# A two-layer encoder trunk: the scan, the projections and attention issued in the order in which the program emits them

## The chip, the cores and the metric

One core of a Trainium2 chip runs the whole program. The metric is the device time of one execution in microseconds (us), taken as the median of three runs. The core has four engines that compute, each with its own queue of instructions: TensorE (PE, matrix products and transposes), VectorE (DVE), ScalarE (ACT) and GpSimd (POOL). SyncE (SP) issues most DMAs.

## The reference

The kernel computes two layers of a streaming encoder on one sequence of 1024 tokens, model width 1024, in float32. What matters of one layer:

```
h    = rms_norm(x) * (1 + sc1) + sh1                # modulation: c_act @ ada_w
proj = h @ w_in                                      # 1024 x 3232, q, k, v and the inputs of the scan
attn = diff_attention(rotary(q), rotary(k), v)       # 4 heads, two softmaxes each, block-causal
rwkv = rwkv7_time_mix(proj[..., 1536:])              # 8 heads of 64, state scan over 1024 steps
x    = x + gt1 * (concat(attn, rwkv) @ w_out)
x    = x + gt2 * hier_moe(rms_norm(x)*(1+sc2)+sh2)   # 32 experts, top 2 of one group
```

The scan is `state = state*w + (state@a)*b + v*k`, `y = state@r`. A final RMSNorm follows the second layer.

## The kernel before

Each layer has two parts. The second part (the experts) is not touched. The first part, `phase_a`, holds the projections, the scan and attention, and is written as a set of generators ("agents") that a small planner, `weave`, steps through.

- The planner keeps a clock. An agent's step emits some instructions and yields two numbers: how much TensorE time the step takes, and how long the agent is to rest afterwards. A yield can also name an event (`"step", n`, `"F", 0`, `"H"`) that the agent waits for. At each turn the planner takes the first agent by rank whose rest is over. Ranks: the scan's second half 0 to 3 (`rwkv_back`, `rwkv_mid`, `rwkv_front`), the solve of the small triangular systems and the scan's first half 4 (`rwkv_first`), turning of q, k and v 5, the projections of the scan 6 (`project`), the modulation of later blocks 7 (`tables`), attention 8, the projections of q, k and v 9 (`head_qkv`).
- The planner charges only TensorE's time. What VectorE and ScalarE take enters as rests (`GAP_R`, `GAP_F`, `GAP_B`, `GAP_S` and so on), as far as a yield stands there.
- The order of emission is not yet the order on the engines. The framework has a scheduler of its own, which runs a timeline by its own cost estimates and puts each engine's instructions in the order in which it finds them ready. Before the change it does so with everything that `weave` emits. In the experts' part, and only there, the helper `in_order` (line 69) chains what it encloses.

Three places are spoken of later:

- A tile of projection weights. `split_w` (line 339) loads 512 KB into `wa_raw`, casts it on ScalarE to `wa_hi` (line 346) and writes the remainder `wa_lo` on VectorE (line 347). `proj_cm` (line 351) then runs, for each of eight blocks of rows, three matmuls: `wa_hi` with `hh`, `wa_hi` with `hl`, `wa_lo` with `hh` (lines 359 to 361), for each half of the tokens. Each finished product is taken out of PSUM by ScalarE: line 1069 for q, k and v, lines 371, 375 and 376 for the inputs of the scan. `wa_hi` and `wa_lo` have two buffers, `wa_raw` one. In `head_qkv` and in `project` no rest stands between the emission of the cast and that of the first matmul.
- The modulation, `ada_ps` (line 238): 512 KB of `ada_w` a step, two buffers, loaded by SP.
- VectorE instructions whose operand comes from a DMA that is issued in the same step: `lam_v` (line 1004, once a layer) and `g2` (line 1279, once a layer, after the load of `n2g` in line 1278).

Of the kernel before, what the change touches and what calls it, by code (L numbers as in the profile page):

```python
# [52 lines left out]
class Trunk:  # L53
# [329 lines left out]
    def weave(self):  # L383

        inf, agents = float("inf"), self.agents

        def ready(x):
            return self.when.get(x, inf) if isinstance(x, (str, tuple)) else x  # L390

        while agents:
            for x in agents:
                if ready(x[2]) <= self.clock:
                    break
            else:
                t = min(ready(x[2]) for x in agents)
                assert t < inf, [x[2] for x in agents]
                self.clock = t
                continue  # L400
            r = next(x[1], None)
            if r is None:
                agents.remove(x)
            elif isinstance(r, tuple) and not isinstance(r[0], str):
                self.clock += r[0]
                x[2] = self.clock + r[1]
            else:
                x[2] = r
# [1590 lines left out]
```

## Time and profile before

| | us |
|---|---|
| runs | 2683.93, 2695.6, 2697.16; median 2695.6 |
| the profiled execution | 2686.03 |
| its span | 2684.2 |
| PE busy | 2370.9 (88%) |
| DVE busy | 1848.7 (69%) |
| ACT busy | 1200.7 (45%) |
| POOL busy | 313.9 (12%) |

Read it by stages. The stretches from 140 to 870 us and from 1450 to 2150 us lie in the first part of the first and of the second layer, where `weave` has emitted the work; the experts run from about 1005 to 1340 and from 2278 to 2613 us. A share of the whole span mixes the two. A wait is the idle time of an engine ahead of an instruction, put down to what ended it. The granted clock of TensorE has two levels, 1.2 and 2.4 GHz; the profile gives its mean as a share of full speed, so 0.50 is the lower level throughout.

### The profile page before, as it was taken

How to read it: one execution, taken by the hardware profiler on the slowest of the kernel's cores; microseconds unless marked ns; L12 is line 12 of the kernel's file. 1: busy time of each engine (PE TensorE's matmuls, PEld its weight loads, DVE VectorE, ACT ScalarE, POOL GpSimd, SP SyncE). 2: the span in 40 equal slices, each digit the busy share in tenths (PEclk: the TensorE clock that was granted, in tenths of full speed). 3: DMA queues.
4: the chain of work that ended last, by engine and by line, in shares of the span. 5: the costliest groups of instructions: out<-in, count | busy, mean ns of one | idle time of the engine just before them, and what ended most of it. 6: DMA issues, size and time to landing. Idle time of an engine off the chain costs nothing. (4 is left out here: it accounts for less than half of the span.)

```text
span 2684.2 us, 45428 instructions
## 1 busy us (share of the span) xinstructions
PE 2370.9 (88%) x17313; PEld 1812.1 (68%) x17313; DVE 1848.7 (69%) x4045; ACT 1200.7 (45%) x2324; POOL 313.9 (12%) x251
## 2 busy tenths in 40 slices
PE   5998998898889969999959989889987996999992
PEld 3676666677767867776737767677776885677771
DVE  3357767656588477877764679965658847887775
ACT  5344443334266225555544545434426622555552
POOL 3000000000000012333310000000000001333330
PEclk8999888889989979999979989899988997999996
DMA  8476665535263258999952434445436234899985
GB/s 300 155 248 201 203 208 164 162 105 143 85 198 100 92 200 293 352 336 363 347 195 80 155 121 134 143 148 156 121 87 204 90 108 186 325 388 348 336 307 201
DMA packets 262789, 542.70 MB, mean 202 GB/s; under 512 B 76376, under 2 KB 180768, under 8 KB 232608
## 3 DMA queue, kind: packets, MB, share of 16 engines
q1 hardware_dynamic: 234560, 484.61, 53.7%
q0 software_dynamic: 23376, 40.99, 4.1%
q10 hardware_dynamic: 4624, 14.06, 1.4%
q8 instruction: 142, 2.33, 0.4%
q14 instruction: 87, 0.71, 0.1%
HBM read 459.29 MB, written 120.09 MB: 216 GB/s over the span
## 5 line engine op out<-in xcount | busy, mean ns | idle before, releaser
L1643 DVE TENSOR_TENSOR w_lo<-w_gu,w_hi 128x2048 fp32r<-128x2048 f32 x134 | 306.4, 2286 | 69.5 <-ACT w_hi L1642 69.3
L1642 ACT CAST w_hi<-w_gu 128x2048 fp32r<-128x2048 f32 x134 | 255.7, 1908 | 211.5 <-PE h_ps L1695 198.3
L359 PE MATMUL pj<-hh,wa_hi 128*128 128x512 f32 x800 | 332.5, 416 | 3.4 <-ACT wa_hi L346 3.1
L360 PE MATMUL pj<-hl,wa_hi 128*128 128x512 f32 x800 | 328.7, 411 | 1.5 <-DVE hl L336 1.4
L361 PE MATMUL pj<-hh,wa_lo 128*128 128x512 f32 x800 | 322.7, 405 | 3.7 <-DVE wa_lo L347 3.6
L1734 PE MATMUL y_ps<-w_d,hT 128*128 128x512 f32 x560 | 252.3, 593 | 3.4 <-ACTq L1795 2.4
L1694 PE MATMUL h_ps<-w_hi,xT_hi 128*128 128x512 f32 x560 | 242.9, 434 | 4.4 <-ACT xT_hi L1678 4.4
L1695 PE MATMUL h_ps<-w_hi,xT_lo 128*128 128x512 f32 x560 | 222.3, 397 | 2.5 <-DVE xT_lo L1679 2.5
L1696 PE MATMUL h_ps<-w_lo,xT_hi 128*128 128x512 f32 x560 | 222.2, 397 | 0.0
L1723 POOL DMA_INDIRECT yd<-yo,idx_s x70 | 183.6, 2624 | 290.2 <-DVE yo L1720 275.4
L359 PEld LDWEIGHTS pj<-hh,wa_hi 128*128 128x128 f32 x800 | 154.2, 193 | 42.9 <-issue 6.3
L361 PEld LDWEIGHTS pj<-hh,wa_lo 128*128 128x128 f32 x800 | 153.7, 192 | 39.6 <-DVE wa_lo L347 5.9
L360 PEld LDWEIGHTS pj<-hl,wa_hi 128*128 128x128 f32 x800 | 154.3, 193 | 36.1 <-issue 3.9
L1734 PEld LDWEIGHTS y_ps<-w_d,hT 128*128 128x128 f32 x560 | 100.9, 190 | 104.8 <-issue 100.4
L1694 PEld LDWEIGHTS h_ps<-w_hi,xT_hi 128*128 128x128 f32 x560 | 107.2, 191 | 38.1 <-issue 11.5
L1695 PEld LDWEIGHTS h_ps<-w_hi,xT_lo 128*128 128x128 f32 x560 | 107.2, 191 | 36.5 <-DVE th L1686 11.5
L1679 DVE TENSOR_TENSOR xT_lo<-xT_ps,xT_hi 128x1024 fp32r<-128x1024 f32 x70 | 85.7, 1225 | 64.8 <-ACT xT_hi L1678 64.8
L1696 PEld LDWEIGHTS h_ps<-w_lo,xT_hi 128*128 128x128 f32 x560 | 106.8, 191 | 23.0
L1720 DVE SCALAR_TENSOR_TENSOR yo<-y_ps,wsl,gt 128x1024 f32<-128x1024 f32 x70 | 89.9, 1284 | 38.3 <-PE y_ps L1734 38.3
L1189 ACT ACTIVATE at_p<-at_s,at_mx 128x256 f32<-128x256 f32 (+7 forms) x128 | 94.9, 741 | 39.0 <-DVE at_mx L1187 38.4
L1187 DVE TENSOR_REDUCE at_mx<-at_s 128x1 f32<-128x256 f32 (+7 forms) x128 | 95.9, 753 | 17.6 <-PE at_s L1185 16.4
L238 PE MATMUL ada_ps<-ada_w,crep 128*32 128x128 f32 x1536 | 70.2, 310 | 41.0 <-DMA ada_w<-in_ada_w 40.9
(436 smaller groups left out, 4934.0 us busy)
## 6 DMA issues: line engine op xcount, KB each, us to landing
w_gu<-in_moe_w_gu SPq DMA_DIRECT2D x140, 1024.0 KB
w_d<-in_moe_w_down SPq DMA_DIRECT2D x70, 1024.0 KB
ada_w<-in_ada_w SPq DMA_DIRECT2D x80, 512.0 KB
wa_raw<-in_w_in SPq DMA_DIRECT2D x50, 512.0 KB
sp_z<-z SPq DMA_DIRECT2D x32, 768.0 KB
b_zz<-sp_z SPq DMA_DIRECT2D x32, 512.0 KB
cy<-yd SPq DMA_DIRECT2D x16, 1024.0 KB
qkv<-qst SPq DMA_DIRECT2D x48, 256.0 KB
```

The costliest lines, as they stand in the source:

```text
L359: nc.tensor.matmul(ps, hi[:, k, :], self.hh[k][:, sl], start=(k == 0), stop=False)
L360: nc.tensor.matmul(ps, hi[:, k, :], self.hl[k][:, sl], start=False, stop=False)
L361: nc.tensor.matmul(ps, lo[:, k, :], self.hh[k][:, sl], start=False, stop=(k == NK - 1))
L1187: nc.vector.tensor_reduce(mx, ps[:, 0:n], axis=AX.X, op=OP.max, negate=True)
L1189: nc.scalar.activation(pm[:, 0:n], ps[:, 0:n], AF.Exp, bias=mx, accum_out=hs["s"][:, t, m:m + 1])
L1642: self.nc.scalar.copy(hi, raw)
L1643: eng.tensor_tensor(lo, raw, hi.bitcast(F32), op=OP.subtract)
L1694: nc.tensor.matmul(ph, hi[:, k, :], whi[:, k % 4, :], start=(k == 0), stop=False)
L1695: nc.tensor.matmul(ph, lo[:, k, :], whi[:, k % 4, :], start=False, stop=False)
L1696: nc.tensor.matmul(ph, hi[:, k, :], wlo[:, k % 4, :], start=False, stop=(k == NK - 1))
L1723: st = nc.gpsimd.indirect_dma_start(out=self.yd, out_offset=bass.IndirectOffsetOnAxis(ap=self.idx_s[:, e:e + 1], axis=0), in_=yos[e % 2], ...
L1734: nc.tensor.matmul(po[:, 512 * half:512 * half + 512], hT[:, k, :], w[:, k, 512 * half:512 * half + 512], start=(k == 0), stop=(k == 1))
```

## The change

Each step of an agent is now taken inside `in_order`, with one record of the last instruction of each engine for the whole of `weave`. Every instruction that a step emits on TensorE, ScalarE, VectorE or GpSimd (DMAs issued by ScalarE and GpSimd among them) gets an ordering edge from the one emitted before it on the same engine. Edges without a semaphore: they add no wait by themselves, they take away the scheduler's choice. SP's queue is not chained, nor is what is emitted before `weave` starts or after it ends.

```diff
-        inf, agents = float("inf"), self.agents
+        inf, agents, self.issued = float("inf"), self.agents, {}
...
-            r = next(x[1], None)
+            with self.in_order(self.issued):
+                r = next(x[1], None)
```

The helper, which both kernels have:

```
    def in_order(self, last):
        engines = [e.engine for e in (self.nc.tensor, self.nc.scalar, self.nc.vector, self.nc.gpsimd)]
        traced = self.nc.cur_bb.bb.instructions
        n = len(traced)
        yield
        for i in traced[n:]:
            if i.engine in engines:
                if i.engine in last:
                    self.tc.add_manual_dep(i, last[i.engine].name, ...)
                last[i.engine] = i
```

Nearly all of TensorE's rows in the first part change place. Lines behind 387 have a number higher by one in the changed kernel. In the rows below a name's last number tells one tile from another of the same name.

ScalarE, first layer, around the cast of the weight tile `wa_hi_6706` (for one of attention's projections). `pj` is the product of a projection in PSUM, `qst` its copy; `at_` is attention, `b_` and `rb_` the scan. Before:

```order
L925 ACTIVATE b_sq_5762<-b_y_5405 128x512
L820 COPY b_tt_5616<-rb_t_5821 32x4x32
L861 COPY b_gg_5790<-rb_m_5792 128x2x64
L346 CAST wa_hi_6706<-wa_raw_6704 128x1024
L1069 ACTIVATE qst_6064<-pj_5865 128x512
L1208 COPY at_wt_6814<-at_t_6815 128x384
L1189 ACTIVATE at_p0_6677,at_sum_6270<-at_s_6671,at_mx0_6675 128x512
```

After:

```order
L821 COPY b_tt_6453<-rb_t_6657 32x4x32
L1190 ACTIVATE at_p0_6677,at_sum_6270<-at_s_6671,at_mx0_6675 128x512
L1070 ACTIVATE qst_6701<-pj_6322 128x512
L346 CAST wa_hi_6706<-wa_raw_6704 128x1024
L1190 ACTIVATE at_p1_6720,at_sum_6270<-at_s_6714,at_mx1_6718 128x512
L840 COPY b_e_6360<-rb_w_6728 128x256
L1029 COPY qst_6739<-qk_t_6740 128x512
```

Before, the cast stands ahead of the copy of an earlier product (`pj_5865`), among work of the scan, with nothing of its own tile's turn in front of it. Now the cast stands directly behind the copy of `pj_6322`, the product that precedes its own use.

TensorE at the first use of the same tile. Before:

```order
L1185 MATMUL at_s_7517<-at_l0_5836,at_q0_6037 128x512
L902 MATMUL rb_y_6338<-b_sb_4417,b_dr_6017 64x128 x4
L908 MATMUL rb_y_6338<-b_e_5784,b_zz_6015 64x64 x16
L804 MATMUL rb_q_6367<-b_tt_6233,b_aa_6231 32x32 x8
L359 MATMUL pj_6710<-hh0_355,wa_hi_6706 128x512
L360 MATMUL pj_6710<-hl0_363,wa_hi_6706 128x512
L361 MATMUL pj_6710<-hh0_355,wa_lo_6707 128x512
L359 MATMUL pj_6710<-hh1_356,wa_hi_6706 128x512
```

After:

```order
L361 MATMUL pj_6322<-hh6_361,wa_lo_6070 128x512
L894 MATMUL rb_s_6693<-b_sb_4417,b_dr_6364 64x64 x2
L359 MATMUL pj_6322<-hh7_362,wa_hi_6069 128x512
L360 MATMUL pj_6322<-hl7_370,wa_hi_6069 128x512
L361 MATMUL pj_6322<-hh7_362,wa_lo_6070 128x512
L359 MATMUL pj_6710<-hh0_355,wa_hi_6706 128x512
L360 MATMUL pj_6710<-hl0_363,wa_hi_6706 128x512
L361 MATMUL pj_6710<-hh0_355,wa_lo_6707 128x512
L1183 MATMUL at_s_6714<-at_k1_5889,at_q1_6109 128x512
```

Before, other work stands ahead of the first matmul with `wa_hi_6706`. Now the last matmul of `pj_6322`, which ScalarE's copy waits for, is the row just ahead of the first matmul that needs the cast behind that copy.

VectorE, first layer, around `g2`, whose operand `n2g` a DMA of the same step brings; `at_mx` are the maxima that attention's exponentials need. Before:

```order
L109 SCALAR_TENSOR_TENSOR rs_y_sub_8606<-rs_u_sub_8607,rs_y_sub_8606 128x4
L107 SCALAR_TENSOR_TENSOR rs_u_sub_8607<-rs_v_sub_8605,rs_y_sub_8606 128x4
L1187 TENSOR_REDUCE at_mx0_8761<-at_s_8755 128x1
L108 TENSOR_TENSOR rs_u_sub_8607<-rs_u_sub_8607,rs_y_sub_8606 128x4
L1196 RECIPROCAL at_rec_8531<-at_sum_8530 128x2
L109 SCALAR_TENSOR_TENSOR rs_y_sub_8606<-rs_u_sub_8607,rs_y_sub_8606 128x4
L1197 SCALAR_TENSOR_TENSOR at_g_8532<-at_sum_8530,nlam_5587,at_rec_8531 128x1
L107 SCALAR_TENSOR_TENSOR rs_u_sub_8607<-rs_v_sub_8605,rs_y_sub_8606 128x4
L1198 SCALAR_TENSOR_TENSOR at_p0_8718<-at_p1_8738,at_g_8532,at_p0_8718 128x512
L108 TENSOR_TENSOR rs_u_sub_8607<-rs_u_sub_8607,rs_y_sub_8606 128x4
```

After:

```order
L109 SCALAR_TENSOR_TENSOR rs_y_sub_8606<-rs_u_sub_8607,rs_y_sub_8606 128x4
L1224 SCALAR_TENSOR_TENSOR at_ob_8425<-at_ob_8425,rs_y_sub_8606,subg_5590 128x128 x4
L1280 SCALAR_TENSOR_TENSOR g2_8652<-g2_8652,n2g_8653 128x1024
L1197 RECIPROCAL at_rec_8531<-at_sum_8530 128x2
L1198 SCALAR_TENSOR_TENSOR at_g_8532<-at_sum_8530,nlam_5587,at_rec_8531 128x1
L1199 SCALAR_TENSOR_TENSOR at_p0_8583<-at_p1_8591,at_g_8532,at_p0_8583 128x256
L1188 TENSOR_REDUCE at_mx0_8686<-at_s_8682 128x1
```

Both stand among attention's instructions. Before, the scheduler has put `g2` where it found the load done, and the maxima `at_mx0_8761` and others ahead of it; now `g2` stands where its step emits it, and the maxima `at_mx0_8686` and all later ones stand behind it.

## Rows read from the trace of the kernel before

**Rows 1.** The page, part 1: busy us, share, instructions.
```profile
PE 2370.9 (88%) x17313; PEld 1812.1 (68%) x17313; DVE 1848.7 (69%) x4045; ACT 1200.7 (45%) x2324; POOL 313.9 (12%) x251
```

**Rows 2.** Windows: stretch, length, busy PE, PEld, DVE, ACT, POOL, clock, DMA, GB/s.
```profile
140.00:870.00 730.00, 651.53 (x6301) 512.84 (x6294) 502.02 (x1424) 318.48 (x815) 11.48 (x27) 0.91 0.54 165
1450.00:2150.00 700.00, 630.59 (x5568) 502.09 (x5567) 507.52 (x1427) 331.94 (x843) 5.74 (x16) 0.93 0.44 132
```

**Rows 3.** Waits of PE, 140 to 870: us in total, times, longest.
```profile
PE rb_s L893 <- DVE b_sb L895: 16.8, 13, 6.7
PE ada_ps L238 <- DMA ada_w<-in_ada_w: 13.2, 11, 3.4
...
PE pj L361 <- DVE wa_lo L347: 3.6, 2, 3.1
...
PE pj L359 <- ACT wa_hi L346: 0.9, 1, 0.9
```

**Rows 4.** Waits of PE, 1450 to 2200.
```profile
PE pj L359 <- ACT wa_hi L346: 2.1, 1, 2.1
```

**Rows 5.** What writes and reads the weight tile: duration ns min/median/max, first and last start.
```profile
L347 DVE TENSOR_TENSOR wa_lo<-wa_raw,wa_hi x50: 1192/1224/1227, 35.1 to 1944.0; 128x1024 fp32r<-128x1024 f32 x50
L346 ACT CAST wa_hi<-wa_raw x46: 1027/1047/1058, 75.8 to 1942.9; 128x1024 fp32r<-128x1024 f32 x46
```

**Rows 6.** Groups of ACT by line, 140 to 870: busy us, mean ns, idle before.
```profile
L1069 ACT ACTIVATE qst<-pj 128x512 f32<-128x512 f32 x24 | 14.3, 597 | 34.0 <-PE pj L361 34.0
L375 ACT ACTIVATE krv<-pj,omu 128x511 f32<-128x511 f32 x9 | 6.1, 682 | 0.0
...
L376 ACT ACTIVATE krv<-pj,carry,omu 128x1 f32<-128x1 f32 x9 | 3.1, 347 | 0.5 <-DVE carry L373 0.5
```

**Rows 7.** Timeline of PE: start, us, instruction, idle before and what ended it.
```profile
229.81 0.49 PE L361 MATMUL pj<-hh,wa_lo 128*128 128x512 f32 x1 [3.12 <-DVE wa_lo L347]
...
230.37 0.40 PE L360 MATMUL pj<-hl,wa_hi 128*128 128x512 f32 x1
230.60 0.40 PE L361 MATMUL pj<-hh,wa_lo 128*128 128x512 f32 x1
...
266.73 1.08 PE L238 MATMUL ada_ps<-ada_w,crep 128*32 128x128 f32 x16 [3.44 <-DMA ada_w<-in_ada_w]
...
1550.26 0.50 PE L359 MATMUL pj<-hh,wa_hi 128*128 128x512 f32 x1 [2.12 <-ACT wa_hi L346]
...
1603.52 0.64 PE L804 MATMUL rb_q<-b_tt,b_aa 32*32 32x32 f32 x16 [2.65 <-DMA b_tt<-tinv]
```

**Rows 8.** Windows behind these waits: columns as in rows 2.
```profile
231.30:234.70 3.40, 3.40 (x10) 2.64 (x9) 3.33 (x11) 1.92 (x7) 0.00 (x0) 0.50 0.57 219
...
1550.30:1554.00 3.70, 3.65 (x15) 2.69 (x16) 3.08 (x7) 2.86 (x5) 0.00 (x0) 1.00 0.33 117
1603.50:1606.90 3.40, 3.38 (x36) 2.91 (x37) 2.08 (x4) 1.63 (x5) 0.00 (x0) 0.50 0.83 245
...
265.50:272.30 6.80, 5.57 (x42) 4.24 (x43) 3.98 (x13) 0.42 (x2) 0.00 (x0) 0.50 1.00 334
```

**Rows 9.** Timeline of SP, two issues of loads of modulation weights.
```profile
260.93 1.04 SPq L235 DMA_DIRECT2D ada_w<-in_ada_w  x2
```

**Rows 10.** Timeline of SP, the load that the second operand of g2 comes by.
```profile
795.49 0.42 SPq L1278 DMA_DIRECT2D n2g<-in_norm_g  x1
```

**Rows 11.** Timeline of DVE: two instructions behind a DMA of their own step.
```profile
801.73 1.23 DVE L1279 SCALAR_TENSOR_TENSOR g<-g,n2g 128x1024 f32<-128x1024 f32 x1 [0.85 <-DMA n2g<-in_norm_g]
...
1768.57 0.29 DVE L1004 TENSOR_TENSOR lam_v<-lam_v 128x128 f32<-128x128 f32 x1 [4.74 <-DMA lam_v<-in_attn_lambda]
```

**Rows 12.** Windows in which the scan's second half runs: columns as in rows 2.
```profile
374.00:700.00 326.00, 286.54 (x3267) 230.73 (x3260) 210.76 (x651) 117.05 (x307) 1.72 (x5) 0.86 0.48 144
...
1600.00:1975.00 375.00, 341.52 (x3628) 270.61 (x3627) 273.13 (x823) 158.90 (x403) 3.92 (x9) 0.94 0.48 142
```

## The prediction

> **What bounds the kernel now.** I read four views in this order. The page's busy shares come first: TensorE is busy for 88% of the span, VectorE for 69% [rows 1]. The windows then say where there is time to win or lose. In the two stretches that the change touches TensorE is busy 651.5 of 730 us and 630.6 of 700 us, so it idles for 78.5 + 69.4 = 147.9 us, and its mean clock is 0.91 and 0.93 [rows 2]. VectorE is at 69 and 73% there, ScalarE at 44 and 47%. TensorE bounds these stretches, but not without holes. Third, the waits: no single one dominates, the largest of the first layer being the scan's state step (16.8 us in 13 waits) and the modulation's loads (13.2 us in 11) [rows 3]. What matters most is a wait that is nearly absent. The projections wait for their weight tiles only 3.6 + 0.9 us in the first layer and 2.1 us in the second [rows 3, 4], because the scheduler has put the casts long before the first use. Fourth, the timeline and the short windows behind single waits, for what a hole costs beyond itself.
>
> **The change, part by part.** It removes and adds no instruction. It fixes four queues to the order of emission, and that order was written with a clock that charges TensorE alone. Where the source has a rest, ScalarE and VectorE have time; where it has none, TensorE arrives too early.
>
> *Weight tiles.* This is the place without a rest. For tile `wa_hi_6706` the order now reads on TensorE: last matmul of the old product, first matmul of the new tile; and on ScalarE: copy of the old product, cast of the new tile. The copy can't start before the last matmul ends, the cast stands behind the copy, and the first matmul needs the cast. So TensorE stands still for the copy and the cast: 0.60 + 1.05 = 1.65 us for a tile of q, k or v, and 0.68 + 0.35 + 1.05 = 2.08 us for one of the scan's inputs, which takes two instructions to copy [rows 5, 6]. Then `wa_lo` follows on VectorE, 1.22 us [rows 5], covered only by the two matmuls that need `wa_hi` alone, 0.23 us apart [rows 7], 0.46 us: another 0.76 us. I went through all tiles in the changed order and counted how much TensorE work stands between the last product that ScalarE must have seen and the first use. In 31 of the 42 tiles of both layers that `weave` emits it is at most 2.1 us, mostly none: 21 of attention's and 10 of the scan's. The others, with 8.7 us and more but for one with 2.4 us, cost nothing. Sum: 21 x 1.65 + 10 x 2.08 = 55.5 us, less about 6.5 us of work that does stand between in some, plus 31 x 0.76 = 23.6 us, makes 73 us; less the 6.6 us that these waits cost before [rows 3, 4], +66 us. Nothing hides it: all four queues are in order, TensorE's next work stands behind the waiting matmul, and the later chains wait for TensorE. The bounds: 49 us if `wa_lo` is always covered; 100 us if each tile takes 1 us more for handing over between engines, the one such wait in the trace lasting 2.12 us with another cast order [rows 7].
>
> *The clock.* The trace shows what a hole does to it. After a wait of 2.12 us the clock stayed at its upper level; after one of 2.65 us and one of 3.12 us it was at the lower one for 3.4 us, and around one of 3.44 us for 6.8 us [rows 7, 8]. At half speed 3.4 us lose 1.7 us. The tiles' holes are 2.4 to 2.8 us, between the one that cost nothing and those that did. I take half of them: 31 x 0.85 = +26 us; the bounds are 0 and 31 x 1.7 = 53 us. The Trainium skill (TensorE: Matmul & The Clock Gate, section "Loop structure matters more than you think") says otherwise: a copy out of PSUM between bursts of matmuls leaves the clock up, and long waits for a DMA take it down. By that rule this term is 0 and the sum 26 us lower; the wait of 3.12 us was for VectorE, not for a DMA, and the trace shows the lower clock behind it, so I don't follow the rule here.
>
> *Loads of their own step.* `g2` came 6.2 us after the issue of its load (795.49 to 801.73), and VectorE idled 0.85 us of that; `lam_v` held VectorE for 4.74 us in the second layer and for nothing in the first [rows 10, 11]. Now both stand where they are emitted, and VectorE stands still until the load has landed, with attention's maxima and the scan's additions behind it. Twice 6.2 and once 4.7 us, less twice 0.85: 15 us of VectorE. TensorE feels it where it has no other work; I take 10 us, bounds 0 and 15.
>
> *Modulation.* The scheduler had spaced its loads so that two of them stand some 7 us of TensorE work apart; in the new order I count 16 loads of the first layer, in two runs of eight, with about 2 us each. With two buffers the third load waits for the first one's use, and a load took 5.8 us from issue to use (260.93 to 266.73) [rows 7, 9]. A run of eight then takes 4 x 5.8 = 23 us and not 16: 2 x 7 = 14 us, and some of the 13.2 us of before [rows 3] go, since those loads stand elsewhere. I take +8 us, bounds -10 and +20.
>
> *All other waits.* 147.9 - 6.6 - 13.2 = 128 us of holes are spread over the scan's and attention's chains. The order of emission runs the scan ahead of its fillers: by TensorE's work its last instruction moves forward by some 35 us in the first layer and 65 us in the second, and attention starts some 55 and 80 us later. Fewer fillers stand between dependent steps, but the rests are there, and each of the 31 holes gives the chains 2.4 us to catch up. I expect a sixth of these waits to go: -20 us. Below, half goes, -64 us; above, they grow by half, +64 us, since VectorE and ScalarE can no longer pass a waiting instruction.
>
> Sum: 66 + 26 + 10 + 8 - 20 = +90 us. Against the profiled execution's 2686.0 us this is 2776 us. That execution lies 9.6 us below the median of the runs and 2 us above their lowest, so half of this is added: 2780 us.
>
> **Rivals.**
> - *The scan ahead of its fillers pays (faster).* While the scan's second half runs the clock is 0.86 and 0.94 [rows 12]: 28% of 326 us and 12% of 375 us at the lower level, worth about 46 + 22 us, and holes of the state step are in the same stretches. If the scheduler's order, which runs fillers early and leaves the scan late, is the cause of both, half of the 128 us of waits and half of the 68 us go: -98 us, against the +66 us of the tiles: about 2655 us. It decides when these two fall by more than the tiles' sum. For it: TensorE is idle for 39 of the 326 us. Against: many of these waits end with the scan's own chain, which keeps its length.
> - *The queues lock into each other (much slower).* VectorE is at 64 to 73% in these stretches [rows 2, 12], and each waiting instruction now stops all behind it. If the 128 us of other waits double and the clock falls at every hole: 66 + 53 + 15 + 20 + 128 = 282 us at the most; half of the doubling and the clock's middle, 66 + 26 + 15 + 12 + 64 = 183 us, is likelier: 2870 us. For it: the planner knows nothing of VectorE's load. Against: the rests are there for just these chains.
> - *The holes are covered (no change).* The chains' waits of before shrink by what the tiles add, because a TensorE that is held up finds its operands ready: 2695 us. For it: 128 us of waits are there to be replaced. Against: the holes fall in the dense stretches of projections, where there are few waits.
> - That the change does nothing is excluded by the order: over 4000 instructions of TensorE in each layer now stand in one rising sequence.
>
> **How the numbers follow.** The forecast has a chance of 0.55, with its own range of 2725 to 2835 us from the bounds of its terms. The lock has 0.25, the cover 0.09, the scan ahead 0.11. The range of all is 2700 to 2875 us: it leaves out the faster case and the upper part of the lock. Half a per cent, 13.5 us, is about what a measurement of this kernel can tell from no change, its three runs lying 13 us apart. Slower by more than that: the forecast and the lock, 0.80. Within: 0.08 of the cover's 0.09, whose last hundredth I put on the faster side. Faster: 0.12.
>
> **What would show it.** In the profile after: TensorE's waits for `wa_hi` at line 359 in the tens, near 50 us in all, and for `wa_lo` at line 361 near 20 us; idle time of the two stretches near 210 us in place of 148; a lower mean clock in the stretches of the projections; `g2` and `lam_v` with some 5 us of idle VectorE each. The experts' stretches unchanged. The prediction is wrong if the waits for weight tiles stay under 30 us, or if they are there and the waits of the scan and attention fall by as much.

## The result: 3206 us instead of 2696, and the profile after

| | before | after |
|---|---|---|
| median of the runs, us | 2696.4 (4 runs, 2683.9 to 2702.9) | 3206.0 (4 runs, 3203.7 to 3212.1) |
| ratio | | 1.190, 95% interval 1.187 to 1.193 |
| span of the profiled execution, us | 2684.2 | 3204.9 |
| TensorE's mean granted clock | 0.926 | 0.859 |

The kernel became slower, as predicted, but by 510 us and not by 90. The page's first part, busy us of each engine (before: [rows 1]):

```profile
PE 2498.5 (78%) x17313; PEld 1867.3 (58%) x17313; DVE 1896.9 (59%) x4045; ACT 1212.9 (38%) x2324; POOL 312.8 (10%) x251
```

The instructions are the same in number. The span grew by 520.7 us. Of these, 127.6 are TensorE's busy time (2370.9 to 2498.5: the same matmuls at a lower clock) and 393 are TensorE's idle time (span less busy: 313 to 706).

The windows say where. The first two rows are the stretches of the two layers that answer to [rows 2], the last two the scan's second half; columns as in [rows 2].

```profile
140.00:1100.00 960.00, 694.65 (x6324) 523.34 (x6322) 526.05 (x1428) 329.25 (x829) 13.18 (x30) 0.83 0.42 127
1700.00:2650.00 950.00, 676.72 (x5376) 513.58 (x5375) 519.02 (x1403) 324.19 (x814) 5.66 (x17) 0.79 0.32 96
503.00:865.00 362.00, 248.51 (x3215) 187.81 (x3214) 179.04 (x541) 87.78 (x227) 1.48 (x8) 0.83 0.33 95
1845.00:2367.00 522.00, 383.10 (x3807) 281.43 (x3807) 276.33 (x812) 141.57 (x353) 3.49 (x12) 0.78 0.31 94
```

In the first two rows TensorE idles for 28 and 29% (before 11 and 10%), at a clock of 0.83 and 0.79 (before 0.91 and 0.93). No engine has become the bound: VectorE fell to 55%. Everybody waits for somebody. The experts take 347 to 348 us from their first to their last transposed block in each layer, as before; nothing of the 510 us is there.

For the scan's second half the windows of [rows 12] are not the right ones to compare with: they end before it does, and the first one begins 39 us too early. By its matmuls it runs, before, in these two stretches:

```profile
412.80:745.50 332.70, 293.51 (x3489) 237.85 (x3489) 200.84 (x627) 107.78 (x281) 2.59 (x10) 0.89 0.43 125
1603.50:2010.20 406.70, 374.30 (x4070) 295.90 (x4070) 288.43 (x882) 164.41 (x419) 3.69 (x12) 0.94 0.45 134
```

So it grew by 29 us in the first layer and 115 us in the second. What comes ahead of it grew by 90 and 12 us, and the stretch from its end to the first expert, where attention is finished, by 110 and 163 us: more than half of the loss lies behind the scan.

The page's groups of the projections (busy, mean ns, idle before and what ended it) and of attention's exponentials; whole program. Before, lines 359 and 361 waited 3.4 and 3.7 us and the exponentials 39.0 us.

```profile
L359 PE MATMUL pj<-hh,wa_hi 128*128 128x512 f32 x800 | 382.4, 478 | 79.3 <-ACT wa_hi L346 79.2
L361 PE MATMUL pj<-hh,wa_lo 128*128 128x512 f32 x800 | 347.3, 434 | 25.1 <-DVE wa_lo L347 24.7
...
L1190 ACT ACTIVATE at_p<-at_s,at_mx 128x256 f32<-128x256 f32 (+7 forms) x128 | 94.6, 740 | 231.4 <-DVE at_mx L1188 231.3
```

TensorE's waits from 140 to 1100 us: us in all, times, longest; answering to [rows 3]. The largest of before, the state step's wait for `b_sb`, is gone from the top; seven others have taken its size.

```profile
PE pj L359 <- ACT wa_hi L346: 29.2, 14, 6.9
PE rb_t L819 <- ACT b_gg L862: 23.6, 3, 7.9
PE rb_s L894 <- issue: 23.0, 4, 11.7
PE at_t L1208 <- ACT at_ob L1218: 22.9, 10, 4.3
PE tp L693 <- DVE z L686: 19.6, 4, 11.9
PE ada_ps L238 <- DMA ada_w<-in_ada_w: 18.3, 12, 3.7
PE rb_m L852 <- DVE b_qt L808: 16.9, 4, 8.2
```

**The step that was predicted.** A weight tile, all engines in order of time (start, us, instruction, idle before it):

```profile
676.64 0.40 PE L361 MATMUL pj<-hh,wa_lo 128*128 128x512 f32 x1
677.13 0.60 ACT L1070 ACTIVATE qst<-pj 128x512 f32<-128x512 f32 x1 [1.42 <-PE pj L361]
...
677.62 1.04 ACT L346 CAST wa_hi<-wa_raw 128x1024 fp32r<-128x1024 f32 x1
678.69 1.23 DVE L347 TENSOR_TENSOR wa_lo<-wa_raw,wa_hi 128x1024 fp32r<-128x1024 f32 x1 [1.45 <-ACT wa_hi L346]
678.71 0.50 PE L359 MATMUL pj<-hh,wa_hi 128*128 128x512 f32 x1 [1.68 <-ACT wa_hi L346]
679.05 0.40 PE L360 MATMUL pj<-hl,wa_hi 128*128 128x512 f32 x1
...
679.97 0.56 PE L361 MATMUL pj<-hh,wa_lo 128*128 128x512 f32 x1 [0.52 <-DVE wa_lo L347]
```

Last matmul of the old product, copy, cast, first matmul of the new one: 1.68 us, then 0.52 us for `wa_lo`, the steps that the prediction drew (1.65 and 0.76 us). Two windows, one over these two waits and one behind them, show the clock falling from the upper to the lower level at 680.3 us; columns as in [rows 8].

```profile
677.00:680.20 3.20, 1.00 (x4) 0.52 (x4) 1.47 (x2) 1.53 (x2) 0.00 (x0) 1.00 0.94 322
680.30:683.60 3.30, 3.30 (x24) 2.45 (x22) 0.44 (x2) 0.00 (x0) 0.00 (x0) 0.50 0.51 182
```

**The step that was not.** The same view around the group norm that ends each half of a head pair (`rwkv_last`); four of the twelve instructions of the reciprocal root (`rs_`) are shown:

```profile
543.20 0.69 DVE L922 TENSOR_REDUCE b_st<-b_y 128x8 f32<-128x512 f32 x1 [3.56 <-ACT b_y L912]
...
543.63 0.72 PE L858 MATMUL rb_m<-b_e,b_zz 64*64 64x64 f32 x30
543.92 0.17 DVE L923 TENSOR_SCALAR b_st<-b_st 128x8 f32<-128x8 f32 x1
544.13 0.69 DVE L924 TENSOR_TENSOR b_y<-b_y,b_st 128x512 f32<-128x512 f32 x1
544.91 0.63 ACT L926 ACTIVATE b_sq<-b_y 128x512 f32<-128x512 f32 x1 [1.75 <-DVE b_y L924]
545.58 0.69 DVE L927 TENSOR_REDUCE b_st<-b_sq 128x8 f32<-128x512 f32 x1 [0.76 <-ACT b_sq L926]
546.30 0.17 DVE L100 TENSOR_SCALAR rs_v_gn<-b_st 128x8 f32<-128x8 f32 x1
546.50 0.17 DVE L104 TENSOR_SCALAR rs_u_gn<-rs_v_gn 128x8 int32<-128x8 int32 x1
...
548.31 0.17 DVE L108 TENSOR_TENSOR rs_u_gn<-rs_u_gn,rs_y_gn 128x8 f32<-128x8 f32 x1
548.51 0.17 DVE L109 SCALAR_TENSOR_TENSOR rs_y_gn<-rs_u_gn,rs_y_gn 128x8 f32<-128x8 f32 x1
548.71 0.69 DVE L929 TENSOR_TENSOR b_y<-b_y,rs_y_gn 128x512 f32<-128x512 f32 x1
...
550.76 0.69 DVE L934 TENSOR_TENSOR b_y<-b_y,b_bo 128x512 f32<-128x512 f32 x1
551.48 0.76 DVE L861 TENSOR_TENSOR b_dr<-rb_m,b_dr 128x256 f32<-128x256 f32 x2
551.94 0.60 ACT L862 COPY b_gg<-rb_m 128x128 f32<-128x128 f32 x2 [6.40 <-DVE b_dr L861]
552.26 0.64 PE L819 MATMUL rb_t<-b_tt,b_qt 32*32 32x32 f32 x16 [7.91 <-ACT b_gg L862]
```

The matmuls `rb_m` end at about 544.3 us. Their read `b_dr` on VectorE is emitted behind the group norm, which runs from 543.20 to 551.45 us in one piece; the copy `b_gg` on ScalarE waits for `b_dr`, and TensorE for `b_gg`: 7.91 us. Nobody needs the result of the group norm in that time: the first instruction that reads it, behind the norm itself, starts at 571.66 us. The norm exists before the change too, but there the scheduler let the same kind of read, `b_dr`, pass between its parts. VectorE's timeline before, at another of the 16 norms:

```profile
554.72 0.69 DVE L921 TENSOR_REDUCE b_st<-b_y 128x8 f32<-128x512 f32 x1 [0.96 <-ACT b_y L911]
555.44 0.42 DVE L860 TENSOR_TENSOR b_dr<-rb_m,b_dr 128x256 f32<-128x256 f32 x1
...
557.42 0.69 DVE L926 TENSOR_REDUCE b_st<-b_sq 128x8 f32<-128x512 f32 x1 [0.76 <-ACT b_sq L925]
558.08 0.42 DVE L860 TENSOR_TENSOR b_dr<-rb_m,b_dr 128x256 f32<-128x256 f32 x1
```

I put every hole of TensorE over 0.25 us down to the work that VectorE and ScalarE mostly did in it (us, first + second layer). Many holes hold work of several kinds, so the rows below the first are rough:

| work in the hole | before | after |
|---|---|---|
| group norm behind the scan | 3.5 + 0.7 | 60.1 + 65.7 |
| attention | 14.6 + 10.5 | 49.2 + 56.5 |
| weight tiles | 0 + 4.3 | 40.1 + 34.7 |
| chain of the scan's first half | 5.8 + 15.0 | 21.8 + 26.9 |
| output weights | 5.4 + 8.5 | 10.6 + 29.2 |

**The clock.** Windows from the end of this hole, columns as in [rows 8]:

```profile
552.20:557.70 5.50, 5.44 (x32) 3.93 (x33) 2.59 (x9) 1.02 (x4) 0.00 (x0) 0.53 0.00 0
557.70:560.50 2.80, 2.80 (x31) 2.10 (x28) 2.60 (x11) 0.59 (x1) 0.00 (x0) 1.00 0.02 6
```

For nearly all of these 5.5 us TensorE ran at the lower level, 1.2 GHz, and lost some 2.6 us beyond the hole (5.5 us at a mean clock of 0.53). What ended the hole was ScalarE's copy, no DMA; the wait of 3.12 us in [rows 7, 8] was ended by VectorE. The clause of the Trainium skill that the prediction weighed (TensorE: Matmul & The Clock Gate, "Loop structure matters more than you think"), that a copy out of PSUM leaves the clock up, would, as it was read there, have put this loss at nothing; the trace does not agree, with a hole of 7.91 us and a clock of 0.53 behind it.

### The profile page after: what moved, and what is told of

It reads as the page before. It is cut to its first block, busy times and chain, and to the rows that moved or that the text cites. A ratio compares the mean times of both kernels' runs of the same rounds, so it can differ in the third digit from the quotient of the medians.

```text
span 3204.9 us, 45368 instructions
## 1 busy us (share of the span) xinstructions
PE 2498.5 (78%) x17313; PEld 1867.3 (58%) x17313; DVE 1896.9 (59%) x4045; ACT 1212.9 (38%) x2324; POOL 312.8 (10%) x251
## 5 line engine op out<-in xcount | busy, mean ns | idle before, releaser
L359 PE MATMUL pj<-hh,wa_hi 128*128 128x512 f32 x800 | 382.4, 478 | 79.3 <-ACT wa_hi L346 79.2
L361 PE MATMUL pj<-hh,wa_lo 128*128 128x512 f32 x800 | 347.3, 434 | 25.1 <-DVE wa_lo L347 24.7
L360 PE MATMUL pj<-hl,wa_hi 128*128 128x512 f32 x800 | 345.0, 431 | 1.6 <-DVE hl L336 1.4
L359 PEld LDWEIGHTS pj<-hh,wa_hi 128*128 128x128 f32 x800 | 167.8, 210 | 135.2 <-ACT wa_hi L346 90.8
L361 PEld LDWEIGHTS pj<-hh,wa_lo 128*128 128x128 f32 x800 | 168.4, 210 | 80.2 <-DVE wa_lo L347 42.1
L360 PEld LDWEIGHTS pj<-hl,wa_hi 128*128 128x128 f32 x800 | 169.4, 212 | 31.8 <-DVE hl L336 3.9
L1208 PE MATMUL at_t<-ident,at_p 128*128 128x128 f32 x288 | 60.2, 328 | 98.2 <-ACT at_ob L1218 58.0
L1183 PE MATMUL at_s<-at_k,at_q 128*128 128x512 f32 (+2 forms) x192 | 89.1, 464 | 50.4 <-DVE at_q L1105 26.7
```

What stands on the lines that cost most here:

```text
L359: nc.tensor.matmul(ps, hi[:, k, :], self.hh[k][:, sl], start=(k == 0), stop=False)
L360: nc.tensor.matmul(ps, hi[:, k, :], self.hl[k][:, sl], start=False, stop=False)
L361: nc.tensor.matmul(ps, lo[:, k, :], self.hh[k][:, sl], start=False, stop=(k == NK - 1))
```

## The experiments

All prices below are differences to the kernel before in the same set of runs, whose medians lie between 2693.7 and 2699.8 us. What a run gives back is the difference of two such prices; the expectations mostly take the plain difference of two medians, which is up to 5 us off. With the change itself the program is 510 us longer. Two helpers serve nearly all experiments: `in_order` takes the list of engines that it chains, and instructions emitted inside `free()` stay out of the chain and are placed by the scheduler.

**1. Which engine's order costs.** Only the list of engines differs:

```diff
-            with self.in_order(self.issued):
+            with self.in_order(self.issued, (self.nc.tensor,)):   # pe_only; scalar: act_only; vector: vec_only
```

- TensorE alone. 

> Only TensorE's instructions are chained in the order of emission; VectorE, ScalarE and GpSimd are left to the scheduler. Theory A (bursts of VectorE and ScalarE work that one step emits at once, group norm and weight tiles first, hold up all that is queued behind them, and TensorE with it): the bursts can be split up and moved again, so the time is near that of before, 2680 to 2800 us. Rival B (TensorE's own new order is what costs: the scan ahead of its fillers leaves its chains uncovered): TensorE's order is that of the changed kernel, so 3000 us or more.


- ScalarE, VectorE and GpSimd, TensorE free. 

> VectorE, ScalarE and GpSimd are chained in the order of emission, TensorE is left to the scheduler. Theory A: the bursts stand as in the changed kernel; TensorE may be given other work around them, so between the two kernels but well above before, 2850 to 3100 us. Rival B: with TensorE's order free again the loss is mostly gone, 2690 to 2800 us.


- VectorE alone. 

> VectorE alone is chained. Theory A: the long bursts are VectorE's, with ScalarE's parts of them waiting in between, so most of the loss: 2950 to 3150 us. Rival D (ScalarE's place behind copies out of PSUM is what costs, by the casts): 2700 to 2800 us.


- ScalarE alone. 

> ScalarE alone is chained. Theory A: the casts of the weight tiles stand behind the copies, which cost some 134 us in the changed kernel, and little else does: 2780 to 2880 us. Rival D: 2950 us or more.

| chained | median, us | more than before, us | ratio, 95% interval |
|---|---|---|---|
| TensorE | 2856.5 | 157 | 1.060 (1.055 to 1.065) |
| ScalarE | 2880.3 | 183 | 1.069 (1.067 to 1.071) |
| VectorE | 3102.3 | 405 | 1.150 (1.148 to 1.152) |
| ScalarE, VectorE, GpSimd | 3236.7 | 537 | 1.199 (1.194 to 1.204) |
| all four (the change) | 3206.0 | 510 | 1.190 (1.187 to 1.193) |

The prices are not a sum: 157 + 183 + 405 = 745 us. VectorE alone and ScalarE alone came out as theory A had it (ScalarE 0.3 us above its range); TensorE alone lies between the ranges of A and B, and the run with TensorE free is slower than both had it. VectorE's order alone costs four fifths of the loss, and once the other three are fixed, TensorE's order adds nothing more; left free, the program is even slower. The prediction looked at the order from TensorE's side; it should have begun with VectorE.

**2. The two steps of the profile above, left out of the chain.**

```diff
-            self.rwkv_last(hp, half, self.yh, self.bo, pool, psum)
+            with self.free():                                   # last_free, both_free
+                self.rwkv_last(hp, half, self.yh, self.bo, pool, psum)
-            return self.split_w(wp, l, c0 // 128, eng=nc.scalar.copy)
+            with self.free():                                   # tile_free, both_free
+                return self.split_w(wp, l, c0 // 128, eng=nc.scalar.copy)
```

- 

> All four engines chained, but what rwkv_last emits (the group norm of half a head pair, 16 times in all) is left out of the chain. Theory A: the 126 us of TensorE's idle time that the trace of the changed kernel shows beside these bursts go, and some of the lower clock with them: 3206 - 126 - 30 = 3050 us, 3010 to 3100. Rival B: the holes lie in the scan's chain, which stays: 3150 to 3206 us.


- 

> All four engines chained, but the casts and remainders of the weight tiles (split_w) are left out of the chain. The prediction's term: TensorE's waits for the tiles were 79.2 + 24.7 us over the whole run in the changed kernel, against 6.6 before; if they go, with 25 us of lower clock, 3206 - 97 - 25 = 3085 us, 3050 to 3130. Theory A adds nothing to this. Rival (the holes are only moved to the next wait): 3150 to 3206 us.


- 

> All four engines chained, but neither the group norm (rwkv_last) nor the weight tiles (split_w). Taken alone these gave back 65 and 134 us of the 510. If the two losses are separate, 3206 - 199 = 3007 us, 2980 to 3035. If one hides behind the other, more comes back than the sum, below 2970 us; if the holes move to the next wait, less, above 3040 us.

Measured: 3140.6 us without the group norm (1.165, 1.159 to 1.170), 3071.9 without the tiles (1.139, 1.133 to 1.144), 3010.7 without both (1.117, 1.115 to 1.119). So the tiles gave back 137 us, as expected, and the group norm 69 us, half of what its holes of 126 us had let me expect, between the ranges of the two theories. Together they gave 197 us, nearly the sum of the two (206): separate losses. With the tiles free their waits are nearly gone:

```profile
L367 PE MATMUL pj<-hh,wa_hi 128*128 128x512 f32 x800 | 367.6, 459 | 6.2 <-ACT wa_hi L354 6.1
...
L369 PE MATMUL pj<-hh,wa_lo 128*128 128x512 f32 x800 | 330.1, 413 | 3.1 <-DVE wa_lo L355 3.1
```

The pages tell idle time from clock. With the group norm free TensorE idles 68 us less, of holes of 126, and is busy as long as in the changed kernel (2499.3 us, there 2498.5). With the tiles free it idles 78 us less, of waits that had grown by 97, and is busy 58 us less (2440.9): the clock. So a hole that goes is in part replaced by the next one, and what the clock adds can be as much again: the time in a hole does not tell what filling it returns.

**3. All such bursts.** I call a burst what a step emits on VectorE and ScalarE in one piece, without a rest. `bursts_free` has `free()` around the two above and also around the norm of k, the chains of the scan's first half, the casts of q, k, v and of the output weights, attention's constants and `open_output` with `g2`; TensorE's instructions in them stay chained.

> All four engines chained, but of VectorE and ScalarE every burst that one step emits without a rest is left out of the chain: group norm, weight tiles, the norm of k, the 20-odd instructions of chain in the scan's first half, the pieces of attention's heads and of the output weights, attention's constants, and g2. Theory A (these bursts are what makes the order of the two vector engines costly): what is left is the cost of TensorE's order, so near the kernel that chains TensorE alone, 2856 us: 2830 to 2930. Rival C (any order fixed on VectorE and ScalarE costs, bursts or not, because the plan knows nothing of their load): 2980 us or more.

Measured: 2930.9 us (1.087, 1.085 to 1.089), 0.9 us above A's range and far from C's. Leaving the bursts out gives back 276 of the 510 us. The 233 us that are left are more than TensorE's order costs alone (157 us), so the bursts are not all.

**4. What TensorE's order costs.** Steps of some agents are left out of TensorE's chain:

```diff
-            with self.in_order(self.issued, (self.nc.tensor,)):
+            with self.in_order(self.issued, (self.nc.tensor,)), self.free(x[1].__name__ == "attention"):   # pe_no_att
```

`pe_no_ada` does so for the modulation, `pe_no_both` for the two, and `pe_scan` for all but the scan's agents.

- 

> TensorE alone is chained, and the steps of the modulation are left out of the chain. With TensorE alone chained the program took 2856 us, 158 more than before; in that run the stretch of the first layer before the scan's second half was 62 us longer than before, and TensorE waited 35 us for modulation weights there in place of 13. Theory M (the modulation's loads, issued in runs of eight with two buffers, make this stretch long): it gets 40 to 60 us shorter, 2795 to 2820 us. Rival (the order of the scan's own first half makes it long): at most the 22 us of the modulation's waits go, 2834 to 2856 us.


- 

> TensorE alone is chained, and the steps of attention (scores, turning of the weights, products with v) are left out of the chain. With TensorE alone chained the stretches from the scan's last instruction to the first expert were 46 us (first layer) and 83 us (second) longer than before. Theory T (attention is put behind the scan's steps and is then left without other work beside it): with attention free the tails shrink by most of this, 2735 to 2790 us. Rival (the tails are long because the projections of q, k and v come late, which attention needs): less than 30 us go, 2826 us or more.


- 

> TensorE alone is chained, and both attention's steps and the modulation's are left out of the chain, so the scan, the projections and the norms remain in it. If these two are the whole price of TensorE's order: 2690 to 2740 us. If the order of the scan and the projections costs something by itself: 2760 us and more.


- 

> TensorE alone is chained, and only the scan's steps (its first half, the solve, the three parts of the second half, the gate) are in the chain; projections, norms, modulation, attention and the output are free. Theory S (the emitted order of the scan's own steps is a good one; with TensorE chained the scan's second half took 314 and 407 us against 333 and 407 before): 2660 to 2700 us, faster than before or equal. Rival (the scan's steps, held to one sequence, stop each other): 2720 us and more.

| left in TensorE's chain | median, us | more than before, us | ratio, 95% interval |
|---|---|---|---|
| all | 2856.5 | 157 | 1.060 (1.055 to 1.065) |
| all but modulation | 2842.2 | 148 | 1.054 (1.052 to 1.056) |
| all but attention | 2806.6 | 112 | 1.042 (1.040 to 1.044) |
| all but both | 2789.9 | 95 | 1.037 (1.034 to 1.039) |
| the scan alone | 2762.9 | 68 | 1.025 (1.023 to 1.027) |

Modulation gave back 9 us, and the run lies in the rival's range: theory M's forecast failed. But its waits, the largest of the first layer in `pe_only`, were not taken away by this. From 140 to 950 us, with all of TensorE chained and with modulation free:

```profile
PE ada_ps L238 <- DMA ada_w<-in_ada_w: 35.1, 18, 4.3
...
PE ada_ps L246 <- DMA ada_w<-in_ada_w: 28.9, 15, 5.4
```

So the run shows that modulation's place in TensorE's chain costs little; what its waits cost it does not show. Attention gave back 45 us, more than the rival allows and less than theory T wanted (the tail of the second layer, from the scan's last matmul to the first expert, went from 343 to 303 us; before 260). And the scan's steps alone, in the order of emission, cost 68 us, against theory S and against the rival of the prediction that hoped for a gain there: the second layer's second half took 442 us in place of 407, and the first layer's part ahead of the second half 302 in place of 266. `pe_no_both` says the same: at 2789.9 us it lies where the order of the scan and the projections costs something by itself. What in the scan's order costs this stays open.

**5. What VectorE's order costs.** The same helpers on VectorE alone.

```diff
+            with self.in_order(self.issued, (self.nc.vector,)):                                         # vec_bursts_free: free() as in bursts_free
+            with self.in_order(self.issued, (self.nc.vector,)), self.free(x[1].__name__ == "attention"):   # vec_no_att
```

- 

> VectorE alone is chained, and its bursts without a rest (group norm, remainders of weight tiles, norm of k, the chains of the scan's first half, pieces of q, k, v and of the output weights, attention's constants, the gain g2) are left out of the chain. With all of VectorE chained alone the program took 3102 us, 404 more than before. Theory B (the bursts are what makes a fixed VectorE dear): 2720 to 2850 us. Rival O (any fixed order of VectorE is dear, since single reads of PSUM and attention's maxima stop each other as well): 2950 us or more.


- 

> VectorE alone is chained, and attention's steps (maxima, sums of the two softmaxes, its norm) are left out of the chain; the bursts stay in it. Theory B: the scan and the projections still stand behind the bursts, only attention can pass them, so a third of the 404 us or less goes: 2970 to 3080 us. Rival O (attention's instructions, which wait for TensorE and ScalarE, are what stops the queue): more than half goes, under 2900 us.


- Both out. 

> VectorE alone is chained, and both the bursts and attention's steps are left out of the chain. Alone, the bursts gave back 180 of the 404 us that VectorE's order costs, attention's steps 137. Theory P (they are separate prices): 404 - 180 - 137 = 87 us are left, 2760 to 2810 us. Rival Q (it is one price, attention standing behind the bursts): what is left is near the 224 us that are left with the bursts free, 2860 us or more.

| left in VectorE's chain | median, us | more than before, us | ratio, 95% interval |
|---|---|---|---|
| all | 3102.3 | 405 | 1.150 (1.148 to 1.152) |
| all but bursts | 2922.2 | 223 | 1.083 (1.081 to 1.085) |
| all but attention | 2965.5 | 266 | 1.099 (1.097 to 1.101) |
| all but both | 2818.5 | 125 | 1.047 (1.043 to 1.051) |

Neither theory of the first two runs came out: bursts returned 182 us, less than B wanted, and attention 139 us, between the two. Together they returned 280, where the two alone add up to 321 us; so they are mostly two prices, with 41 us in common (the run lies between P and Q, nearer P). Attention's part is seen in TensorE's largest wait of `vec_only` from 140 to 1100 us, for the sum of the two softmaxes; it was 3.9 us before, from 140 to 870 us:

```profile
PE at_t L1208 <- DVE at_p L1199: 36.5, 13, 9.1
```

**6. A rest in place of freedom.** All four engines stay chained, but the group norm becomes an agent of its own. With it the step that reads its result rests 6 us in place of 12, and the last part of the next half waits for the norm's event:

```diff
-            self.rwkv_last(hp, half, self.yh, self.bo, pool, psum)
+            self.add(0.5, self.rwkv_last(hp, half, self.yh, self.bo, pool, psum))
...
+        yield 0.0, 2.0                    # ahead of b_sq
+        yield 0.0, 1.5                    # ahead of the sum of squares
+        yield 0.0, 2.0                    # ahead of the product with the root
```

> All four engines are chained as in the changed kernel, but the group norm behind the scan is no longer emitted in one piece: it is an agent of its own with rests of 2.0, 1.5 and 2.0 us between its parts, and the next half's last part waits for its event. Theory B (what fails is a burst without a rest, not the fixed order as such): rests do what leaving it out of the chain did (3141 us): 3090 to 3165 us. Rival O: the fixed order costs the same wherever the pieces stand: 3190 us and more.

Measured: 3124.5 us (1.158, 1.156 to 1.161), in theory B's range: 85 us less than the change and 16 less than with the norm free, the last at the edge of the noise. VectorE's timeline shows other work between its parts:

```profile
554.95 0.17 DVE L109 SCALAR_TENSOR_TENSOR rs_y_gn<-rs_u_gn,rs_y_gn 128x8 f32<-128x8 f32 x1
555.04 0.37 DVE L749 TENSOR_TENSOR sv_m<-sv_t,sv_n 64x220 f32<-64x220 f32 x1
...
556.65 0.42 DVE L839 COPY b_w<-rb_w 128x256 f32<-128x256 f32 x1
...
557.68 0.68 DVE L932 TENSOR_TENSOR b_y<-b_y,rs_y_gn 128x512 f32<-128x512 f32 x1
```

So the fixed order as such is not what costs at this place, but what the emission puts in one piece. No version with a chain beat the kernel before; the nearest, the scan on TensorE alone, is 2.5% slower.

## Why the prediction was right in sign and wrong in size

- **Weight tiles, +66 us: right in mechanism and count, too small in size.** TensorE waited for `wa_hi` 31 times, for 21 tiles of attention and 10 of the scan, as counted. Ten of attention's waits are 1.62 to 1.68 us (worked out: 1.65) and four of the scan's 1.95 (2.08). But the five longest are 4.5 to 13.4 us, 34 us together: in three of them ScalarE's copy or cast stood behind the chain of the scan's first half (11 instructions of VectorE in 4.2 us, and ScalarE's behind them), in one behind a group norm, the constants of attention and a DMA, in one behind attention's output. That the waits for `wa_lo` come out as summed (24.7 us, worked out: 23.6) is luck: there were 22 and not 31, twelve of them of 0.52 to 0.53 us in place of 0.76, and seven of 1.1 to 4.5 us made up for it. Both waits make 103.9 us in place of 73, and with the tiles free 137 us came back, against 66 and the 26 of the clock.
- **The clock, +26 us: too small.** The prediction let half of the tiles' holes take the clock down, for 3.4 us each. It fell during 23 of the 31 waits for `wa_hi` or within 4 us behind them, for 3.4 to 10.2 us each and once for 20.5; how much of this other holes near them did is not told apart. The run with the tiles free puts their share at 58 us of busy time, above the bound of 53. Over the program TensorE's busy time grew by 128 us, since the other holes do the same: the one of 7.91 us cost some 2.6 us behind it.
- **Loads of their own step, +10 us: too large on VectorE, too small on TensorE.** VectorE stood still 3.0 and 4.1 us ahead of `g2` (worked out: 6.2 each), 8.0 us for `lam_v` in the first layer (4.7) and not at all in the second, where a group norm now runs right up to it. That is 15.1 us in all, but 6.4 us stood there before (0.85 twice and 4.74), so 8.7 us were added where 15 was worked out. The rows answer to [rows 11]:

```profile
621.03 0.29 DVE L1005 TENSOR_TENSOR lam_v<-lam_v 128x128 f32<-128x128 f32 x1 [8.01 <-DMA lam_v<-in_attn_lambda]
...
991.29 1.22 DVE L1280 SCALAR_TENSOR_TENSOR g<-g,n2g 128x1024 f32<-128x1024 f32 x1 [3.02 <-issue]
```

  TensorE's holes beside them were 11.7, 8.0 and 9.1 us, 29 in all, above the bound of 15: what stands ahead of the wait and behind it on VectorE counts too.
- **Modulation, +8 us: near in size.** Its waits went from 13.2 to 18.3 us. Whether the two runs of eight loads made this, as the prediction had it, no run shows.
- **All other waits, -20 us: this step failed.** TensorE's idle time grew by 393 us; less 97 of the tiles (103.9 less 7 before), 29 of the loads and 5 of modulation, some 260 us stand where -20 was forecast. The sentence behind it, "the rests are there", holds for the scan's state step, whose wait for `b_sb` fell out of the top (of its other 23.0 us there, 11.7 are the hole beside `lam_v`). It does not hold inside the group norm (8.25 us of VectorE in one piece), the chain of the first half (4.2 us) and the other bursts of experiment 3, for which the planner's clock counts nothing: a rest holds back the agent that yields it, but what other agents emit in the meantime stands in the queue behind the piece. I had looked for places without a rest on the path of the weight tiles only.
- **The rival "the queues lock into each other"** was the right one in kind, and its reason ("the planner knows nothing of VectorE's load") is what experiments 3, 5 and 6 bear out. Its price was capped at 282 us by doubling the waits of before. A wait that doesn't exist before can't be had by scaling those that do.
- **The scan ahead of its fillers** did not pay: even with TensorE alone chained the scan's second half gained 19 us in the first layer (314 in place of 333) and nothing in the second, and the stretches around it lost more. Its price was taken from the windows of [rows 12]; in the right ones the lower clock is worth some 61 us and not 68, which changes little.

What stays open: why the scan's own order costs 68 us on TensorE, what makes up the last 125 us of VectorE's order, what the 233 us are that remain with all four engines chained and the bursts free, and how the prices of the engines overlap.

## What to carry to other kernels

Before a queue is fixed to the order of emission, list for every engine what one step emits on it in one piece. Here pieces of 1 us (a cast) to 8 us (the group norm) that nobody needed at once held up the reads that stood behind them, and in the one place where it was tried, rests inside the piece gave back 85 us. Look for the loss in these pieces, not in the waits that the old profile shows, since the old order has them hidden. Number times length is a rough first size: 16 norms of 8.25 us are 132 us, and 69 came back; the tiles gave back more than their waits, by the clock. Chain one engine at a time when the whole costs: here VectorE's order cost 405 us, TensorE's 157 us, and the prices did not add.

## What the runs showed of the hardware

Nothing that was not in the trace before, but more of it: a hole of 7.91 us ended by ScalarE was followed by 5.5 us at a mean clock of 0.53, waits of 1.68 and 0.52 us by 3.3 us at 0.50, and over the program the same 17313 matmuls were busy for 2498.5 us in place of 2370.9, at a mean clock of 0.859 in place of 0.926.
